# Shifting where the blocks of three operands begin in SBUF, in a two-layer trunk with experts

## The chip, the cores and the metric

The kernel runs on one core of one Trainium2 chip. The metric is the device time of one execution in microseconds (us). All times come from one profiled execution of the kernel before, and from three timed runs of it.

## The reference

Two decoder layers run over 256 tokens of width 1024, in float32. Each layer is an adaLN-modulated RMSNorm, a token mixer (latent attention and forgetting attention side by side), a gated residual, a second modulated RMSNorm, a channel mixer, and a gated residual; a final RMSNorm ends it. What matters here are the two channel mixers:

```
def swiglu(h, w_gate, w_up, w_down):
    return (jax.nn.silu(h @ w_gate) * (h @ w_up)) @ w_down

# layer 0: dense, h is (256, 1024), the hidden width is 3584
f = swiglu(h, dense_w_gate[0], dense_w_up[0], dense_w_down[0])

# layer 1: each token goes to the best 2 of 8 experts, gates is (256, 8)
for e in range(8):
    y = y + gates[:, e:e+1] * swiglu(t, w_gate[e], w_up[e], w_down[e])
```

## The kernel before, in words

**Numbers.** Every large product is made in three float32r matmuls. A float32 value is split into a part `hi` (rounded to float32r by ACT) and the rest `lo` (by DVE), and `hi*hi + hi*lo + lo*hi` is summed in PSUM. `mm3` (L392 to L395) does this for three given operands, and `wide` and `down` write it out for the experts. In `nc.tensor.matmul(out, a, b)` the second argument is the stationary operand, 128 columns of it, loaded by an own weight load, and the third is the moving operand, which streams through with 256 or 512 columns. Each matmul has its own weight load, also where two in a row load the same block.

**Weights from memory.** A `Stream` brings all weights in the order in which they are used. SP issues a DMA of up to 2048 columns into a buffer `raw` (L142), ACT makes `whi` of it (L160), DVE makes `wlo` (L181), and PE uses the two. A DMA waits until its buffer is free again, that is until `wlo` has been made of what lay there. The order is written out by hand in `early_order` and `moe_order`; `pump`, `rest`, `idle` and `get` decide how far ACT and DVE run ahead of PE.

**The dense stage** (`dense`, layer 0). The tokens, turned so that the width lies on the partitions, are `dT_hi` and `dT_lo`: 8 blocks of 256 columns each, block k for the 128 features k. For each of 28 slices of the hidden width, `column_products` makes gate and up: weight block k (128 columns of `whi` or `wlo`) is stationary and token block k (256 columns of `dT_hi` or `dT_lo`) is moving, three matmuls for each k. The first slice goes through `first_products`. Then the activations `dg_hi` and `dg_lo` are stationary and the down weights move, with 512 columns.

**The experts' stage** (`experts`, layer 1). `gather` collects up to 128 tokens of an expert with matmuls against a selection matrix and puts them, turned, into tiles `xe0` to `xe7`: tile k holds for two experts the `hi` and the `lo` block of features k, four blocks of 128 columns (512 bytes in each partition). `wide` makes gate and up in chunks of 512 hidden columns (7 chunks for each expert): here the tokens `xe` are stationary and the weights move with 512 columns; for each k there are three matmuls, `hi*whi`, `hi*wlo`, `lo*whi`. `turn` transposes the activations of a chunk (L1054) and splits them into `g_hi` and `g_lo`, four blocks of 128 columns each. `down` has block f of `g_hi` or `g_lo` stationary and the down weights moving, 6 matmuls for each f, into `ps_y` (L1071). For the last chunk of the last expert, `turn` takes tiles named `xe0` and `xe2` instead of `g_hi` and `g_lo`.

**Where tiles lie.** Pools hand out addresses in the order in which tiles are first asked for. Small unused tiles (`gap`) stand between some of them. In the built program every float32r operand, stationary or moving, begins at a multiple of 512 bytes in its partition, except half of the latent value weights (L734): their moving operand is eight runs of 64 columns, which begin at 256 bytes past such a multiple.

Of the kernel before, what the change touches and what calls it, by code (L numbers as in the profile page):

```python
# [15 lines left out]
F32R = mybir.dt.float32r  # L16
# [7 lines left out]
P = 128  # L24
D = 1024
KD = D // P
S = 256
# [9 lines left out]
NFC = FC // P  # L37
# [5 lines left out]
CAP = P  # L43
# [15 lines left out]
HELD = ((1, 2), (1, 5))  # L59
SPLIT_BUFS = 4  # L60
LAST = 2

NATURAL = ((0, 1), (2, 3), (4, 5), (6, 7))
PAIRS = ((0, 2), (1, 3), (4, 6), (5, 7))
# [175 lines left out]
def trunk_kernel(ctx: ExitStack, tc: tile.TileContext, x, c, positions, w_early, w_moe, router_w,  # L240
# [18 lines left out]
    def bank(tag, shape, name):  # L259
        return psum.tile(shape, F32, tag=tag, name=name, bufs={"A": 4, "B": 2, "C": 2}[tag])  # L260
# [223 lines left out]
    def close(l, section, acc, parts, n, table=None, spare=None, pairs=PAIRS, early=0):  # L484

        ps = [bank(tag, [P, 2, S], "ps_nt") for tag in ("BCBC" if pairs is PAIRS else "BBCC")]
        rs, dg = [], []
        for b in range(NB):  # L490
            ss = tiny.tile([P, 2], F32, name="ss", bufs=4)
            for j in range(0 if b else early):
                for c in halves:
                    parts(j, b, c)
            for i, c in enumerate(halves):
                for j in range(0 if b else early, n):
                    parts(j, b, c)
                t = scratch([P, 512], F32, "gated")
                nc.vector.tensor_mul(t, acc[b][i], rows[l, section][:, c])
                nc.vector.tensor_add(x_sb[:, b, c], x_sb[:, b, c], t)  # L500
                square_sum(x_sb[:, b, c], ss[:, i:i + 1])
                if b and not i:
                    dg.append(diag(rs[0]))
            rs.append(row_r(ss, D, "x", ws.rest if b else None))
        dg.append(diag(rs[1]))
        if table:
            nc.scalar.preload_act_table_set(table)
        sums = ws.held.pop(spare)() if spare else iter(())
        bank_was, fold_bank[0] = fold_bank[0], "A"
        for b in range(NB):  # L510
            turned(x_sb, b, dg[b], ps, pairs)
            for put in islice(sums, 1):
                ws.late.append([partial(tuple, (put,)), 2])
        fold_bank[0] = bank_was
        return ps, rs
# [43 lines left out]
    def mixer(l, pool, ps_x, loads=None, steps=None):  # L559
# [217 lines left out]
        def group_T(g, between=None):  # L777

            ps = [bank("A" if g else "B", [P, 2, S], "ps_nt") for _ in range(2)]
            for b in range(NB):  # L780
                turned(o_sb[g], b, o_dg[g][b], ps)

            def high(kk, j):
                i = 4 * g + 2 * kk + j
                nc.scalar.activation(onT_hi[:, i], ps[kk][:, j], AF.Copy, scale=vec(l, V_OUT + i, 1))

            def low(kk, j):
                i = 4 * g + 2 * kk + j
                nc.vector.scalar_tensor_tensor(onT_lo[:, i], ps[kk][:, j], vec(l, V_OUT + i, 1),
                                               onT_hi[:, i].bitcast(F32), ALU.mult, ALU.subtract)  # L790


            for kk in range(2):
                for j in range(2):
                    high(kk, j)
                for j in range(2):
                    low(kk, j)
                    if between and not kk + j:
                        between()
# [8 lines left out]
        def out_first(kd):  # L808
            if not acc:
                acc.extend([bank("A", [P, 512], "ps_w") for _ in range(2)] for _ in range(NB))  # L810
            w = ws.get()
            for b in range(NB):
                for hf in range(2):
                    out_part(kd, w, b, halves[hf], kd == 4, False)
# [22 lines left out]
        group_T(0, partial(ws.pump, 1, SPLIT_BUFS))  # L837
        for kd in range(4 - LAST):
            out_first(kd)
        last = ws.get(LAST)  # L840
        ws.settle(True)
        if l:
# [3 lines left out]
        ws.pump(2 - l, need=2)  # L846
        return close(l, 2, acc, lambda i, b, c: out_part(4 - LAST + i, last[i], b, c, False, i == LAST - 1), LAST,
                     "silu_and_others" if l == 0 else None, pairs=NATURAL if l else PAIRS)


    def dense(l, pool, ps_x):
        hT_hi = pool.tile([P, KD, S], F32R, name="dT_hi")
        hT_lo = pool.tile([P, KD, S], F32R, name="dT_lo")
        modulated_T(l, V_FFN, 4, 3, ps_x, hT_hi, hT_lo)
        acc = [[bank("A", [P, 512], "ps_d") for _ in range(2)] for _ in range(NB)]
        fold_bank[0] = "C"
        gs = {}

        def down(j, w, b, c):
            t = slice(b * P, (b + 1) * P)  # L860
            mm3(acc[b][c.start // 512], gs[j][0][:, t], gs[j][1][:, t], w[0][:, c], w[1][:, c], j == 0, j == NF - 1)

        for j in range(NF):
            if j:
                ps = bank("B", [P, 2, S], "ps_gu")
                ps = ps[:, 0], ps[:, 1]
                for i in range(2):
                    column_products(hT_hi, hT_lo, ps[i])
                    ws.idle(2)
            else:  # L870
                ps = bank("B", [P, S], "ps_gu"), bank("C", [P, S], "ps_gu")
                first_products(hT_hi, hT_lo, ps)
                ws.idle(4)
            if 0 < j < NF - LAST + 1:
                w = ws.get()
                for b in range(NB):
                    for hf in range(2):
                        down(j - 1, w, b, halves[hf])
                ws.idle(2)
            if j == NF - 1:  # L880
                ws.rest()
            s = pool.tile([P, S], F32, name="silu", bufs=2)
            nc.scalar.activation(s, ps[0], AF.Silu)
            nc.vector.tensor_mul(s, s, ps[1])
            g_hi = pool.tile([P, S], F32R, name="dg_hi", bufs=LAST + 1)
            g_lo = pool.tile([P, S], F32R, name="dg_lo", bufs=LAST + 1)
            split(g_hi, g_lo, s)
            gs[j] = (g_hi, g_lo)
        last = ws.get(LAST)
        ws.settle(True)  # L890
        ws.pump(1, need=2)
        nc.scalar.preload_act_table_set("natural_log_exp_and_others")
        fold_bank[0] = "B"
        return close(l, 5, acc, lambda i, b, c: down(NF - LAST + i, last[i], b, c), LAST, spare=(1, 2), early=LAST - 1)


    def experts(l, outer, ps_x, rs):
# [11 lines left out]
        w = outer.tile([P, 4, NB], F32, name="w")  # L909
# [6 lines left out]
        back, xe = {}, {}  # L916
# [87 lines left out]
        with tc.tile_pool(name="moe", bufs=1, reuse_waits="tile") as pool:  # L1004
            def gather(e, pk):

                xe[e], xe[e + 1] = [], []
                for k0 in range(0, KD, 2):
                    for k in range(k0, k0 + 2):
                        both = pool.tile([P, 2, 2, CAP], F32R, name=f"xe{k}")  # L1010
                        ps = bank("B", [P, 2, 2, CAP], "ps_g")
                        for i, part in enumerate((h_hi, h_lo)):
                            for b in range(NB):
                                nc.tensor.matmul(ps[:, i], part[:, b, k * P:(k + 1) * P], pk[:, b],  # L1014
                                                 start=(b == 0), stop=(b == NB - 1))
                        nc.scalar.activation(both, ps, AF.Copy)
                        for j in range(2):
                            xe[e + j].append((both[:, 0, j], both[:, 1, j]))
                    yield
# [20 lines left out]
            def turn(pend):  # L1040
                e, ch, act = pend
                g = []
                yield e, ch, g
                if (e, ch) == (E - 1, CH - 1):

                    spare = [pool.tile([P, 2, 2, CAP], F32R, name=f"xe{f}") for f in range(0, NFC, 2)]
                    groups = [(2 * i, 2 * i + 2, [t[:, 0], t[:, 1]]) for i, t in enumerate(spare)]
                else:
                    groups = [(0, NFC, [pool.tile([P, NFC, CAP], F32R, name=f"g_{w}") for w in ("hi", "lo")])]
                for f0, f1, (hi, lo) in groups:  # L1050
                    n = f1 - f0
                    ps = bank("B", [P, n, P], "ps_gt")
                    for i in range(n):
                        nc.tensor.transpose(ps[:, i], act[:, (f0 + i) * P:(f0 + i + 1) * P], ident)  # L1054
                    split(hi[:, :n], lo[:, :n], ps)
                    g += [(hi[:, i], lo[:, i]) for i in range(n)]
                    yield
# [434 lines left out]
```

## Time and profile before

| | |
|---|---|
| median of 3 runs | 1524.0 us (1523.59 to 1524.49) |
| profiled execution | 1524.38 us |
| its span, first to last instruction | 1522.2 us |
| granted TensorE clock, mean over the span | 0.995 |
| dense stage | about 155 to 390 us |
| experts' stage | about 538 to 1511 us |

PE is TensorE's matmul, PEld its weight load, DVE VectorE, ACT ScalarE, SP SyncE with the DMA queue. Matmuls are pipelined: the duration of a matmul is its latency, and the next one starts long before it ends. The pace of PE is therefore read from one start to the next, never from the duration. Where a row is merged (x2, x24), its start is that of the first matmul in it. Starts are rounded to 0.01 us, so that a pace is taken over several matmuls.

### The profile page before, as it was taken

To read this page: it belongs to the slowest core of one execution; us is meant where nothing else is said; L and a number is where in the kernel's file an instruction comes from. 1 tells how busy PE (TensorE), PEld (TensorE's weight loads), DVE (VectorE), ACT (ScalarE), POOL (GpSimd) and SP (SyncE) were. 2 spreads that over 40 slices of the span, in tenths; PEclk is the share of its full clock that TensorE was granted. 3 is DMA by queue.
4 is the path that set the end of the run, shared out by engine and by line. 5 is a ranking of instruction groups with operands and counts; after the bars stand their busy time and mean duration, and the time that the engine had idled before them with its cause. 6 is when DMAs were issued, how large, how long until landed. Compare 5 with 4: busy or idle time off the path is not lost.

```text
span 1522.2 us, 20572 instructions
## 1 busy us (share of the span) xinstructions
PE 1491.9 (98%) x7985; PEld 1277.0 (84%) x7985; DVE 1265.4 (83%) x1209; ACT 1004.9 (66%) x1068; POOL 12.6 (1%) x20
## 2 busy tenths in 40 slices
PE   8999999999999899999999999999999999999997
PEld 7988999999898678888888888888888888888885
DVE  5988877777776678899889889879889888988987
ACT  5575544444657576777677777677777777776774
POOL 1000000000000000000000000000000000000000
PEclk9999999999999999999999999999999999999999
DMA  9974778778581269999999999999999998999992
GB/s 373 412 268 166 290 276 309 287 291 299 186 291 56 84 257 363 378 364 371 366 347 348 373 367 366 371 340 347 377 370 368 373 362 324 369 372 377 360 370 91
DMA packets 68472, 481.73 MB, mean 316 GB/s; under 512 B 7953, under 2 KB 8593, under 8 KB 10770
## 3 DMA queue, kind: packets, MB, share of 16 engines
q1 hardware_dynamic: 68178, 480.33, 83.1%
q8 instruction: 63, 1.03, 0.3%
q14 instruction: 39, 0.32, 0.1%
q0 software_dynamic: 192, 0.05, 0.0%
HBM read 479.25 MB, written 1.05 MB: 316 GB/s over the span
## 4 chain that ended last, share of the span: by engine, by line
PE 63%; DVE 1%; ACT 0%; issue 0%; DVEq 0%; ACTq 0%
PE ps_y L1071 20%; PE ps_gate L1028 20%; PE ps_up L1028 19%; PE ps_gt L1054 2%; PE ps_g L1014 1%; DVE wlo L181 0%; PE ps_sc L1097 0%; PE ps_sc L1098 0%; ACT whi L160 0%; PE ps_sc L1121 0%; PE ps_b L928 0%; DVE fin L1129 0%; ACT L1154 0%; DVE gate L347 0%; ACT junk L399 0%
## 5 line engine op out<-in xcount | busy, mean ns | idle before, releaser
L181 DVE TENSOR_TENSOR wlo<-raw,whi 128x2048 fp32r<-128x2048 f32 (+1 forms) x474 | 923.8, 1975 | 62.5 <-ACT whi L160 57.2
L160 ACT ACTIVATE whi<-raw 128x2048 fp32r<-128x2048 f32 (+1 forms) x474 | 769.9, 1662 | 158.6 <-PE ps_gu L394 77.4
L1028 PE MATMUL ps_gate<-whi,xe 128*128 128x512 f32 x896 | 301.8, 396 | 0.0
L1028 PE MATMUL ps_up<-whi,xe 128*128 128x512 f32 x896 | 288.3, 390 | 0.0
L1028 PEld LDWEIGHTS ps_up<-whi,xe 128*128 128x128 f32 x896 | 168.3, 188 | 35.3
L1028 PEld LDWEIGHTS ps_gate<-whi,xe 128*128 128x128 f32 x896 | 168.3, 188 | 33.4
L1028 PE MATMUL ps_gate<-wlo,xe 128*128 128x512 f32 x448 | 175.1, 391 | 0.7 <-DVE wlo L181 0.7
L1028 PE MATMUL ps_up<-wlo,xe 128*128 128x512 f32 x448 | 174.9, 390 | 0.1
L1071 PE MATMUL ps_y<-wlo,g_hi 128*128 128x512 f32 x440 | 136.8, 389 | 0.4 <-DVE wlo L181 0.4
L1071 PE MATMUL ps_y<-whi,g_hi 128*128 128x512 f32 x440 | 136.7, 389 | 0.0
L1071 PE MATMUL ps_y<-whi,g_lo 128*128 128x512 f32 x440 | 136.6, 389 | 0.0
L393 PE MATMUL ps_gu<-dT_hi,whi 128*128 128x256 f32 x432 | 122.5, 284 | 0.0
L395 PE MATMUL ps_gu<-dT_hi,wlo 128*128 128x256 f32 x432 | 122.2, 283 | 0.0
L394 PE MATMUL ps_gu<-dT_lo,whi 128*128 128x256 f32 x432 | 122.2, 283 | 0.0
L444 ACT ACTIVATE g_hi<-ps_gt 128x512 fp32r<-128x512 f32 x55 | 33.0, 599 | 127.1 <-PE ps_gt L1054 127.1
L1028 PEld LDWEIGHTS ps_up<-wlo,xe 128*128 128x128 f32 x448 | 84.1, 188 | 19.0 <-DVE wlo L181 1.4
L1028 PEld LDWEIGHTS ps_gate<-wlo,xe 128*128 128x128 f32 x448 | 84.3, 188 | 17.0 <-DVE wlo L181 1.3
L1071 PEld LDWEIGHTS ps_y<-wlo,g_hi 128*128 128x128 f32 x440 | 82.4, 188 | 18.0 <-DVE wlo L181 1.0
L445 DVE TENSOR_TENSOR g_lo<-ps_gt,g_hi 128x512 fp32r<-128x512 f32 x55 | 37.9, 689 | 71.4 <-ACT g_hi L444 71.4
L1071 PEld LDWEIGHTS ps_y<-whi,g_lo 128*128 128x128 f32 x440 | 82.6, 188 | 17.2
L1071 PEld LDWEIGHTS ps_y<-whi,g_hi 128*128 128x128 f32 x440 | 82.3, 188 | 16.9
L393 PEld LDWEIGHTS ps_gu<-dT_hi,whi 128*128 128x128 f32 x432 | 82.8, 192 | 1.2 <-issue 0.2
(295 smaller groups left out, 1926.4 us busy)
## 6 DMA issues: line engine op xcount, KB each, us to landing
raw<-in_w_moe_dram SPq DMA_DIRECT2D x336, 1024.0 KB, 6.9
raw<-in_w_early_dram SPq DMA_DIRECT2D x114, 1024.0 KB, 6.8
raw<-in_w_early_dram SPq DMA_DIRECT2D x6, 512.0 KB, 8.6
gate<-in_ada_b_dram SPq DMA_DIRECT2D x4, 512.0 KB, 5.6
x_sb<-in_x_dram SPq DMA_DIRECT2D x1, 1024.0 KB, 7.3
out_dram<-fin SPq DMA_DIRECT2D x4, 256.0 KB, 2.0
fg<-in_final_g_dram SPq DMA_DIRECT2D x1, 512.0 KB, 4.9
cn<-in_consts_dram SPq DMA_DIRECT2D x1, 192.0 KB, 12.6
```

The source lines that it names most:

```text
L160: self.nc.scalar.activation(hi, raw, AF.Copy)
L181: self.nc.vector.tensor_sub(parts[1], raw, parts[0].bitcast(F32))
L393: nc.tensor.matmul(out_, lh, rh, start=start, stop=False)
L394: nc.tensor.matmul(out_, lh, rl, start=False, stop=False)
L395: nc.tensor.matmul(out_, ll, rh, start=False, stop=stop)
L444: nc.scalar.activation(hi, src, AF.Copy)
L445: nc.vector.tensor_sub(lo, src, hi.bitcast(F32))
L1014: nc.tensor.matmul(ps[:, i], part[:, b, k * P:(k + 1) * P], pk[:, b], start=(b == 0), stop=(b == NB - 1))
L1028: nc.tensor.matmul(ps, lh, w[:, c], start=(k == 0 and lh is xe_hi and w is hi), stop=(k == KD - 1 and lh is xe_lo))
L1054: nc.tensor.transpose(ps[:, i], act[:, (f0 + i) * P:(f0 + i + 1) * P], ident)
L1071: nc.tensor.matmul(y_ps[e][hf], lh, w[:, hf * 512:(hf + 1) * 512], start=(ch == 0 and f == 0 and lh is g_hi and w is hi), stop=(last and l ...
```

## The change

The change makes three groups of blocks begin at different places within 512 bytes. `STEP` is 16 float32 elements, 64 bytes.

- `dT_hi` and `dT_lo` get rows of 256 + 16 elements for each block, of which 256 are used. Block k then begins 64 k bytes past a multiple of 512. These are moving operands.
- Tile `xe{k}` grows from 2048 to 2560 bytes in a partition, and its four blocks begin 64 k bytes into it. All eight tiles begin at multiples of 512, so the blocks of features k begin 64 k bytes past one. These are stationary operands.
- `g_hi` and `g_lo` get rows of 128 + 16 elements, so that block f is 64 bytes further on than the one before. Each of these tiles has then 2304 bytes. In the built program `g_hi` begins at a multiple of 512 and `g_lo`, which follows it, 256 bytes past one: its blocks lie at 256, 320, 384 and 448. These are stationary operands. For the last chunk the two spare `xe` tiles are used from their beginning.

The weights `whi` and `wlo` stay at multiples of 512. The built programs have the same instructions in the same order on every engine, with the same sizes and the same waits; only addresses and strides differ.

```
+STEP = 16
...
     def dense(l, pool, ps_x):
-        hT_hi = pool.tile([P, KD, S], F32R, name="dT_hi")
-        hT_lo = pool.tile([P, KD, S], F32R, name="dT_lo")
+
+        hT_hi, hT_lo = (pool.tile([P, KD, S + STEP], F32R, name=f"dT_{w}")[:, :, :S] for w in ("hi", "lo"))
...
                     for k in range(k0, k0 + 2):
-                        both = pool.tile([P, 2, 2, CAP], F32R, name=f"xe{k}")
+                        both = pool.tile([P, 4 * CAP + KD * STEP], F32R, name=f"xe{k}")
+                        both = both[:, k * STEP:k * STEP + 4 * CAP].rearrange("p (w j s) -> p w j s", w=2, j=2)
...
-                    spare = [pool.tile([P, 2, 2, CAP], F32R, name=f"xe{f}") for f in range(0, NFC, 2)]
+                    spare = [pool.tile([P, 4 * CAP + KD * STEP], F32R, name=f"xe{f}")[:, :4 * CAP]
+                             .rearrange("p (w j s) -> p w j s", w=2, j=2) for f in range(0, NFC, 2)]
                     groups = [(2 * i, 2 * i + 2, [t[:, 0], t[:, 1]]) for i, t in enumerate(spare)]
                 else:
-                    groups = [(0, NFC, [pool.tile([P, NFC, CAP], F32R, name=f"g_{w}") for w in ("hi", "lo")])]
+                    groups = [(0, NFC, [pool.tile([P, NFC, CAP + STEP], F32R, name=f"g_{w}")[:, :, :CAP]
+                                        for w in ("hi", "lo")])]
```

## Rows read from the trace of the kernel before

**Rows 1.** The page: span, busy time by engine, chain by engine.
```profile
span 1522.2 us, 20572 instructions
PE 1491.9 (98%) x7985; PEld 1277.0 (84%) x7985; DVE 1265.4 (83%) x1209; ACT 1004.9 (66%) x1068; POOL 12.6 (1%) x20
PE 63%; DVE 1%; ACT 0%; issue 0%; DVEq 0%; ACTq 0%
```

**Rows 2.** Two stretches: us, busy by engine (x instructions), clock, DMA share, GB/s.
```profile
155.00:390.00 235.00, 234.58 (x1663) 220.67 (x1663) 180.18 (x225) 109.30 (x144) 0.00 (x0) 1.00 0.80 295
545.00:1510.00 965.00, 963.86 (x4398) 796.86 (x4397) 850.11 (x522) 701.70 (x491) 0.00 (x0) 1.00 0.93 354
```

**Rows 3.** The chain in order of time: start us, us, what (x count).
```profile
558.68 5.44 PE ps_up L1028 x24
575.48 5.46 PE ps_up L1028 x24
...
751.21 5.44 PE ps_y L1071 x24
```

**Rows 4.** Timeline of PE, dense gate and up: start us, us, instruction.
```profile
350.80 0.28 PE L395 MATMUL ps_gu<-dT_hi,wlo 128*128 128x256 f32 x1
...
352.12 0.28 PE L394 MATMUL ps_gu<-dT_lo,whi 128*128 128x256 f32 x1
```

**Rows 5.** Timeline of PE, from 256 to 512 columns and back (dense down).
```profile
347.46 0.40 PE L393 MATMUL ps_d<-whi,dg_hi 128*128 128x512 f32 x1
347.69 0.40 PE L394 MATMUL ps_d<-wlo,dg_hi 128*128 128x512 f32 x1
...
348.85 0.39 PE L393 MATMUL ps_d<-whi,dg_hi 128*128 128x512 f32 x1
...
350.21 0.28 PE L393 MATMUL ps_gu<-dT_hi,whi 128*128 128x256 f32 x1
350.32 0.28 PE L394 MATMUL ps_gu<-dT_lo,whi 128*128 128x256 f32 x1
350.44 0.28 PE L395 MATMUL ps_gu<-dT_hi,wlo 128*128 128x256 f32 x1
```

**Rows 6.** Timeline of PE, latent values, moving operand 256 bytes off.
```profile
102.12 0.39 PE L394 MATMUL ps_uv<-wlo,cq_hi 128*128 128x512 f32 x1
...
103.28 0.38 PE L746 MATMUL ps_t<-cn,pr 128*128 128x128 f32 x2
```

**Rows 7.** Line L954: duration ns min/median/max, first and last start us.
```profile
L954 PE MATMUL ps_r<-rw,rT x32: 275/275/275, 523.0 to 526.5; 128*128 128x128 f32 x32
```

**Rows 8.** Groups by shape: xcount | busy us, mean ns | idle before us.
```profile
L1028 PE MATMUL ps_gate<-whi,xe 128*128 128x512 f32 x896 | 301.8, 396 | 0.0
L1028 PE MATMUL ps_up<-wlo,xe 128*128 128x512 f32 x448 | 174.9, 390 | 0.1
L1071 PE MATMUL ps_y<-whi,g_lo 128*128 128x512 f32 x440 | 136.6, 389 | 0.0
L393 PE MATMUL ps_gu<-dT_hi,whi 128*128 128x256 f32 x432 | 122.5, 284 | 0.0
```

**Rows 9.** Waits of the DMA queue: us in total, times, longest us.
```profile
SPq L142 <- DVE wlo L181: 1123.4, 394, 19.0
```

**Rows 10.** The page's 40 slices: GB/s that the DMA engines moved.
```profile
GB/s 373 412 268 166 290 276 309 287 291 299 186 291 56 84 257 363 378 364 371 366 347 348 373 367 366 371 340 347 377 370 368 373 362 324 369 372 377 360 370 91
```

## The prediction

> **What bounds the kernel now.** I read the page first. PE is busy for 98% of the span, and the chain that ended last, which reaches back to the start of the experts' stage, is almost all PE [rows 1]. The table by stretches says the same stage by stage: in the dense stage PE is busy for 234.58 of 235 us, and in the experts' stage for 963.86 of 965, at a granted clock of 1.00, the 2.4 GHz level [rows 2]. So what one matmul costs from start to start is what these two stages cost, and nothing else that the change touches is on the path.
>
> Then I read that pace from starts. In the experts' stage 24 matmuls of 512 columns take 5.44 to 5.46 us, 226.7 ns each, for gate and up and for down alike [rows 3]. In the dense stage eleven matmuls of 256 columns take 352.12 - 350.80 = 1.32 us, 120.0 ns each [rows 4]. The difference, 106.7 ns, is what 256 columns cost. So 512 columns cost 213.3 ns, and in both shapes 13.3 ns are left over for each matmul: 226.7 - 213.3 and 120.0 - 106.7. This rest doesn't grow with the columns. It belongs to what each matmul has once, and that is its weight load, which runs while the matmul before it streams.
>
> The rest is not the same everywhere. In the dense down products the first six matmuls after the switch from 256 columns take 348.85 - 347.46 = 1.39 us, 231.7 ns each, and the next six 350.21 - 348.85 = 1.36, 226.7. On the way back the first 256-column matmul takes 350.32 - 350.21 = 0.11 us and the next 0.12 [rows 5]. The weight load and the stream therefore meet in some way that depends on how they stand to each other, and settle after a few matmuls into the pace that the stages run at. Whether that meeting is one of addresses is the question that the change asks. 13.3 ns are 32 columns of 4 bytes, 128 bytes of the moving operand's stream, twice the 64 bytes of a step.
>
> **The change part by part.** The instructions, their order, sizes and waits stay. What could change is the pace of the matmuls whose stationary or moving block is shifted, and the writing of those blocks. The writes (ACT and DVE into `dT`, `xe`, `g`) have as many elements as before, in `dT` and `g` with 64 bytes left out behind each block; they lie beside PE, and I cost them at nothing: DVE is busy for 850 of 965 us and ACT for 702 [rows 2]. Without that cover a slower `g_lo` would delay `down`, which comes a chunk later, so it has many microseconds to spare.
>
> The number of shifted matmuls, of the groups in [rows 8] (each line has its fellows): gate and up of the experts are 2 x (896 + 448) = 2688, of which blocks k = 1 to 7 are shifted, 2352. Down has 3 x 440 = 1320; `g_hi` is stationary in two thirds of them and shifted for three of four blocks, 660, and `g_lo` is shifted in all 440. Dense gate and up have 3 x 432 and 48 more in the first slice, 1344, of which 1176 are shifted.
>
> What one shift is worth no row shows for float32r at other than multiples of 512 and 256 bytes. The bounds:
> - Best: the whole rest of 13.3 ns goes. (2352 + 1100 + 1176) x 13.3 = 62 us.
> - Worst: the matmuls never settle, and run at the 231.7 ns seen after a switch: 5.0 ns more on the experts' 2688 + 1320 matmuls, 20 us, and nothing in the dense stage, where the unsettled matmul was the faster one.
> - Nothing: 0.
>
> For a start 256 bytes off there is a row: the latent values' moving operand begins there, and five matmuls take 103.28 - 102.12 = 1.16 us. The same five behind a switch with everything at multiples of 512 take 348.85 - 347.69 = 1.16 [rows 5, 6]. So a distance of 256 bytes buys nothing, and I take the blocks at 256 out: k = 4 in gate and up (336 matmuls) and in the dense stage (168), and f = 0 of `g_lo` (110). 2016 + 990 + 1008 = 4014 matmuls are left.
>
> For these I take half of the rest, 6.7 ns: it is what the one 256-column matmul with another footing saved (0.11 us against 0.12, and 106.7 + 6.7 = 113.4), it is one step of 64 bytes at the stream's pace, and it lies between nothing and all. 4014 x 6.7 = 26.9 us: 6.8 in the dense stage, 20.1 in the experts'.
>
> Is it handed back? The experts' stage would shrink from 965 to 945 us. DVE would then be busy for 850 of 945, 90%. The DMA would have to bring 354 x 965 / 945 = 362 GB/s on average; single slices of this stage already run at 378 and an early one at 412 [rows 10]. The DMA queue mostly waits for a buffer, 1123 us in total for DVE's `wlo` [rows 9], so it is the user and not the memory that sets its pace. I hand back 1 us. In all -26: the profiled execution took 1524.4 us (a span of 1522.2 and 2.2 around it, 0.4 over the median), and 1524 - 26 = 1498.
>
> The Trainium skill speaks against this. In "TensorE: Matmul & The Clock Gate", section "Step-by-step: what each phase is for", it says that PE has two independent read ports to SBUF and that loading the next weights doesn't take read bandwidth from the running matmul. By that the rest is no meeting of two reads, and the sum is 0: this is the first rival. The section "Back-to-back issue gap" there gives N/2.4 + 2.5 ns, 215.8 ns for 512 columns; this trace has 226.7, so something that this rule doesn't hold takes 10.8 ns of each. By the rule's pace as a floor the best case would be 4628 x 10.8 = 50 us.
>
> **The rivals.**
> 1. Nothing happens; the rest is a fixed price of a float32r weight load. For it: the rest is the same for all tiles, wherever they lie, and in both shapes; the 256-byte start made no difference [rows 6]; and the router's 32 matmuls, whose moving blocks begin at 32 k bytes past a multiple of 512, all have the same duration, 275 ns at the least and at the most, and take some 113 ns each [rows 7]. Against it: those are plain float32, streaming at a slower pace per column, and the rest varies behind a switch. Time: 1524.
> 2. Slower: the settled pace needs the stationary and the moving block to keep their relation from one matmul to the next. Block k changes it after every three matmuls of gate and up and every two or four of down, and the unsettled stretch behind a switch lasts about six [rows 5], so the experts' stage stays unsettled at 231.7 ns: +20 us, 1544. It decides if L1028 runs above 229 ns on average. For it: among the 512-column rows of the dense down products the settled ones are the fastest. Against it: it takes the disturbance of a switch for that of an address, and rows 6 show none.
> 3. All of the rest goes for all shifted blocks: -62 us by count, 46 of them in the experts' stage, which would then want 354 x 965 / 919 = 372 GB/s and DVE at 92.5%. That is as much as most slices reach; I hand back 10 us: 1472.
>
> **How the numbers follow.** A measurement of this kernel tells 0.2%, 3 us, from no change. Forecast (a gain of 8 to 40 us, 1498 as the middle): 0.34. Rival 3: 0.08. Rival 1, within 3 us: 0.31. Rival 2, and lesser losses of the same kind: 0.27. So faster 0.42, same 0.31, slower 0.27. The forecast's own range is 1484 to 1516. The range for 8 in 10 has to hold rival 1 and most of rival 2: 1478 to 1544 leaves out some 0.06 below and 0.11 above, where losses beyond the 5 ns lie.
>
> **What would show it.** The pace from start to start by block: in `wide`, k = 0 and 4 should stay at 226.7 ns and the other k be at 220; in the dense gate and up 113 against 120; in down `g_lo` f = 0 should be as before. If all k have the same pace as before, rival 1 holds. If k = 0 is slower too, the disturbance is carried from block to block, as in rival 2. The forecast is wrong too if the pace falls and the time doesn't: then PE must show new idle time in front of L1028 and L1071, ended by DVE's `wlo`.

## The result and the profile after

The changed kernel is slower: 1538.0 us (median of 4 runs, 1536.85 to 1540.09) against 1524.0 beside it, a ratio of 1.0093 (95% interval 1.0076 to 1.0111), +14.0 us. The forecast was 1498.

The page of the profile shows the same kernel with a slower PE. The profiled execution is the slowest of the four: its span grew by 15.6 us, and PE's busy time by 15.5. DVE and ACT, the instructions and the chain's shares are all but the same as in [rows 1].

```profile
span 1537.8 us, 20573 instructions
PE 1507.4 (98%) x7985; PEld 1277.3 (83%) x7985; DVE 1265.9 (82%) x1209; ACT 1005.0 (65%) x1068; POOL 12.6 (1%) x20
PE 64%; DVE 1%; ACT 0%; issue 0%; DVEq 0%; ACTq 0%
```

The stretches show where. The columns are those of [rows 2]; the experts' stretch is taken 15 us longer, so that it holds the same 4398 matmuls. PE is busy for all of both at the same clock, so the 15 us are a slower pace. DMA falls from 354 to 349 GB/s, because the same bytes have more time.

```profile
155.00:391.00 236.00, 235.58 (x1681) 221.00 (x1681) 181.37 (x227) 110.99 (x147) 0.00 (x0) 1.00 0.80 296
545.00:1525.00 980.00, 979.16 (x4398) 797.65 (x4397) 850.52 (x522) 702.54 (x491) 0.00 (x0) 1.00 0.92 349
```

The chain in order of time, which answers to [rows 3], gives that pace: 24 matmuls of 512 columns take 5.56 us, 231.7 ns each, in gate and up and in down, where they took 5.44 to 5.46.

```profile
576.41 5.56 PE ps_up L1031 x24
581.97 5.56 PE ps_y L1076 x24
...
610.62 5.56 PE ps_up L1031 x24
```

The dense timeline, which answers to [rows 4], has thirteen intervals in 352.56 - 351.02 = 1.54 us, 118.5 ns, where there were 120.0. It has got faster, by 1.5 ns and not by 6.7.

```profile
351.02 0.28 PE L396 MATMUL ps_gu<-dT_lo,whi 128*128 128x256 f32 x1
...
352.56 0.28 PE L397 MATMUL ps_gu<-dT_hi,wlo 128*128 128x256 f32 x1
```

The groups by shape, to be held against [rows 8], go the same two ways. These are latencies and not paces: the three 512-column groups have a mean of 2 to 4 ns more, the 256-column group 3 ns less.

```profile
L1031 PE MATMUL ps_gate<-whi,xe 128*128 128x512 f32 x896 | 305.1, 400 | 0.0
L1031 PE MATMUL ps_up<-wlo,xe 128*128 128x512 f32 x448 | 175.8, 392 | 0.0
L1076 PE MATMUL ps_y<-whi,g_lo 128*128 128x512 f32 x440 | 138.2, 393 | 0.0
L395 PE MATMUL ps_gu<-dT_hi,whi 128*128 128x256 f32 x432 | 121.3, 281 | 0.0
```

The waits show no new one. The longest wait of PE for DVE's `wlo` in front of L1031 is 0.6 us, and the DMA queue waits a little longer for its buffers than in [rows 9], since PE now takes them more slowly.

```profile
PE ps_gate L1031 <- DVE wlo L183: 0.6, 1, 0.6
SPq L144 <- DVE wlo L183: 1140.7, 394, 19.0
```

Added up from start to start over the whole trace, gate and up of the experts take 9.2 us more (2688 matmuls, 3.4 ns each), down 6.3 us more (1344, 4.7 ns each), and the dense gate and up 2.0 us less (1344, 1.5 ns each). That is +13.5 of the 15.6 us by which the span of this execution grew. Of the rest, 0.4 us lie in the dense down products and 1.7 in small products, most of them outside the two stages.

### The profile page after: what moved, and what is told of

Its sections match the earlier page's. It is cut to its first block, busy times and chain, and to the rows that moved or that the text cites. A ratio compares the mean times of both kernels' runs of the same rounds, so it can differ in the third digit from the quotient of the medians.

```text
span 1537.8 us, 20573 instructions
## 1 busy us (share of the span) xinstructions
PE 1507.4 (98%) x7985; PEld 1277.3 (83%) x7985; DVE 1265.9 (82%) x1209; ACT 1005.0 (65%) x1068; POOL 12.6 (1%) x20
## 3 DMA queue, kind: packets, MB, share of 16 engines
q8 instruction: 63, 1.03, 0.3%
## 4 chain that ended last, share of the span: by engine, by line
PE 64%; DVE 1%; ACT 0%; issue 0%; DVEq 0%; ACTq 0%
PE ps_y L1076 20%; PE ps_gate L1031 20%; PE ps_up L1031 20%; PE ps_gt L1059 2%; PE ps_g L1017 1%; DVE wlo L183 0%; PE ps_sc L1102 0%; PE ps_sc L1103 0%; PE ps_sc L1126 0%; PE ps_b L930 0%; ACT whi L162 0%; DVE fin L1134 0%; ACT L1159 0%; DVE gate L349 0%; ACT junk L401 0%
## 5 line engine op out<-in xcount | busy, mean ns | idle before, releaser
L1031 PE MATMUL ps_gate<-whi,xe 128*128 128x512 f32 x896 | 305.1, 400 | 0.0
L1031 PE MATMUL ps_up<-whi,xe 128*128 128x512 f32 x896 | 292.1, 394 | 0.0
L1031 PEld LDWEIGHTS ps_up<-whi,xe 128*128 128x128 f32 x896 | 168.2, 188 | 38.8
L1031 PEld LDWEIGHTS ps_gate<-whi,xe 128*128 128x128 f32 x896 | 168.8, 188 | 36.5
L1031 PE MATMUL ps_gate<-wlo,xe 128*128 128x512 f32 x448 | 175.8, 392 | 0.6 <-DVE wlo L183 0.6
L1031 PE MATMUL ps_up<-wlo,xe 128*128 128x512 f32 x448 | 175.8, 392 | 0.0
L1031 PEld LDWEIGHTS ps_up<-wlo,xe 128*128 128x128 f32 x448 | 84.3, 188 | 19.8 <-DVE wlo L183 1.4
L1031 PEld LDWEIGHTS ps_gate<-wlo,xe 128*128 128x128 f32 x448 | 84.6, 189 | 17.3 <-DVE wlo L183 1.0
```

Source lines behind the costliest of these rows:

```text
L1031: nc.tensor.matmul(ps, lh, w[:, c], start=(k == 0 and lh is xe_hi and w is hi), stop=(k == KD - 1 and lh is xe_lo))
```

## The experiments

The question was what in an address sets the pace. "Distance" below is the start of the stationary block minus that of the moving block, in bytes within a partition. So a moving block that begins 112 bytes further on has a distance of -112, which is 144 modulo 256. In the expectations A is the theory that a change of place from one block to the next costs (rival 2 of the prediction), B that the absolute place costs (a block that doesn't begin at a multiple of 512 bytes), C that addresses do nothing to a matmul and the time comes from the writing of the blocks, D that the distance counts, modulo 256 bytes.

**1. Places one by one.** A kernel of nothing but float32r matmuls in groups of 36 with one pair of places in each (all other work left out):

```
+    for i, (n, moves) in enumerate(TESTS):
+        for j, (s0, m0) in enumerate(moves):
+            nc.tensor.matmul(ps[:, :n], st[:, s0:s0 + P], mv[:, m0:m0 + n], ...)
```

> Only a row of float32r matmuls, 36 in each group, back to back, none waits for data; the rest of the trunk is left out. Groups differ in where the stationary block (128 columns) and the moving block (512 or 256 columns) begin. Theory A (a matmul's pace hangs on whether the relation of its start addresses to those of the matmul before stays): with any constant offset the pace settles at 226.7 ns (120.0 for 256 columns), as with none; with an offset that changes from matmul to matmul it runs unsettled at 229 to 236. Theory B (a block that doesn't begin at a multiple of 512 bytes costs more by itself): a constant offset costs the same 232. Theory C (addresses do nothing, the longer time comes from the writing side): 226.7 in all groups. Theory D (the relation of the stationary to the moving block sets the price): constant offsets of one of the two differ among each other, offsets of both by the same amount don't.

Four stretches of its timeline (start us, us from the first start to the last end, count): distance 0, distance 64, distance 256, and both blocks 64 bytes off.

```profile
16.69 4.49 PE L299 MATMUL ps_t<-mv,st 128*128 128x512 f32 x19
...
48.74 5.53 PE L299 MATMUL ps_t<-mv,st 128*128 128x512 f32 x23
...
81.66 5.60 PE L299 MATMUL ps_t<-mv,st 128*128 128x512 f32 x24
...
173.84 5.38 PE L299 MATMUL ps_t<-mv,st 128*128 128x512 f32 x23
```

With the last one's latency of 0.40 us taken off, one takes (4.49 - 0.40) / 18 = 227 ns, 233, 226 and 226. The means over the last 24 of each group, worked out from the starts (the very first group over its last 12, as its first starts are still 427 ns apart):

```
512 columns, stationary block moved by   0: 226.7   64: 233.3  128: 232.7  192: 228.9  256: 226.7
                                       320: 233.3  384: 232.1  448: 228.9
512 columns, moving block moved by      16: 231.7   64: 228.9  256: 226.7  384: 233.3  448: 233.3
both moved by                           64: 226.7  256: 226.7
stationary place 64 bytes on each time, or after every three: 231.7; 256 or 512 bytes on each time: 226.7
both places on together each time by    64: 230.5  128: 228.3  448: 231.7  256: 226.7
256 columns, stationary block moved by   0: 120.0   64: 117.8  128: 118.6  192: 117.8  256: 120.0  320: 113.3
distance 0, other widths, columns      384: 173.3  448: 206.7  480: 216.7  496: 223.3
```

For 512 columns, a moving block 64 bytes on does what a stationary one 64 bytes back does (228.9 both), 320 does what 64 does, and if both lie 64 bytes on nothing happens. So the distance counts, modulo 256 bytes, as D says. A constant 64 doesn't come back to 226.7, which A wanted, and both off by 64 costs nothing, against B. C falls too, because nothing writes these blocks while the matmuls run. The stepping pattern of the change gives 231.7, the pace of `wide` after.

The distance of a matmul's own two blocks is not all of it, however. Where both places go on together from one matmul to the next, by 64, 128 or 448 bytes, that distance is 0 throughout, and yet the matmuls run slower than 226.7 ns:

```profile
338.76 6.62 PE L299 MATMUL ps_t<-mv,st 128*128 128x512 f32 x28
...
346.83 6.56 PE L299 MATMUL ps_t<-mv,st 128*128 128x512 f32 x28
...
363.72 6.65 PE L299 MATMUL ps_t<-mv,st 128*128 128x512 f32 x28
```

These are (6.62 - 0.40) / 27 = 230 ns, 228 and 231. So a change of place does cost something, as A says, unless it is one of 256 bytes. For 256 columns one distance had two paces (117.8 at 64, 113.3 at 320), and that stays unexplained.

**2 to 4. The parts of the change alone.** Each is one part of the diff (the notes behind `#`, here and below, are not in the code):

```
+        hT_hi = pool.tile([P, KD, S + STEP], F32R, name="dT_hi")[:, :, :S]           # dense alone
+                        both = both[:, k * STEP:k * STEP + 4 * CAP].rearrange(...)   # xe alone
+    groups = [(0, NFC, [pool.tile([P, NFC, CAP + STEP], F32R, ...)[:, :, :CAP] ...   # g alone
```

> Only dT_hi and dT_lo are shifted. In the kernel with all shifts the dense gate and up run at about 118.7 ns instead of 120.0: 1344 x 1.3 = 1.8 us faster by theories A and D, 1522.2; not slower. Theory B: slower, by up to 4 us. Theory C: 1524.

1523.49 us against 1523.49, ratio 0.9997 (0.9988 to 1.0006). The dense gate and up are 1.9 us shorter in its trace, less than the time can tell: inconclusive by the time.

> Only the experts' tokens are shifted. Theory A: L1028 runs unsettled at 231.7 ns, and the groups of down that follow it settle within some six matmuls: 2688 x 4 = 10 to 12 us slower, about 1535. Theory B: 2352 of 2688 matmuls slower by 5, 12 us, and down exactly as before at 226.7 from its first matmul on. Theory C: slower only if PE shows idle time in front of L1028.

1532.71, ratio 1.0055 (1.0040 to 1.0071). In its chain gate and up have slowed, and down almost not:

```profile
564.63 5.46 PE ps_y L1075 x24
576.08 5.56 PE ps_up L1031 x24
```

> Only g_hi and g_lo are shifted. Theory A: down unsettled at about 231.5 ns, 1320 x 4.8 = 6 us slower, about 1530, and the first matmuls of gate or up behind each down slower too. Theory B: 990 x 5 = 5 us slower and gate and up as before. Theory C: slower only by idle time in front of L1071.

1530.95, ratio 1.0047 (1.0032 to 1.0062), and here only down:

```profile
559.28 5.44 PE ps_up L1030 x24
564.72 5.54 PE ps_y L1073 x24
```

The parts give +9.2, +7.5 and 0, together 16.7 against the whole's 14.0, with intervals of some 2.5 us on each. The loss is that of the two stationary operands. A slow product slows the other one only where it begins: with `xe` alone shifted, the first four matmuls of each down take 236, 228, 232 and 231 ns (medians) and the others 227, which is 1.1 us over all of down.

**5. Every 16 bytes, and bfloat16.** The same kind of kernel, with 30 in a group, each distance twice and behind different groups (the loop is that of experiment 1), and 120 matmuls of bfloat16:

```
+    for i, r in enumerate((0, 32, 64, 96)):
...
+            nc.tensor.matmul(ps, sb[:, r:r + P], mb[:, :512], start=(j == 0), stop=(j == 29))
```

> Again only matmuls, the rest of the trunk is left out. Float32r with 512 and with 256 columns, the distance of the stationary from the moving block in steps of 16 bytes from 0 to 240, each once behind matmuls of the other shape and once behind 480-column ones; then the dense stage's own pattern, 12 of 512 columns with both at multiples of 512 and 48 of 256 columns with the moving block at a constant distance; then bfloat16 at four distances. The theory so far (the price is set by the distance of the two blocks modulo 256 bytes): the same mean for a distance whatever came before, 512 columns 226.7 at 0, about 233 at 64, 128 to 233 at 128, 229 at 192; 256 columns 120.0 at 0 and lower elsewhere, 113.3 at the best. Rival (each distance has several paces and what came before chooses): the two passes differ. For bfloat16, which reads half the bytes, either the same steps at all distances or none.

512 columns ran at 233.3 ns for most distances, at 226.7 at 0, 228.9 at 192 and 228.3 at 240, in both passes alike to 0.6 ns. 256 columns ran at 120.0 at 0 and settled at 113.3 with the moving block 112 bytes on, in both passes; 32 gave 116.7, most others 117 to 120. But at some places the passes differ: 118.7 and 116.7 ns at 16 bytes, 118.8 and 117.3 at 160. There the rival of the expectation holds, that what came before chooses among several paces. The timeline shows 256 columns at 0, then at 112, and the bfloat16 matmuls at 0, 64, 128 and 192 bytes together:

```profile
273.74 3.52 PE L290 MATMUL ps_t<-mv,st 128*128 128x256 f32 x28
...
312.83 1.41 PE L290 MATMUL ps_t<-mv,st 128*128 128x256 f32 x11
...
570.42 26.07 PE L296 MATMUL ps_b<-mb,sb 128*128 128x512 bf16 x117
```

(3.52 - 0.28) / 27 = 120.0 and (1.41 - 0.28) / 10 = 113.0. The bfloat16 row has 117 records of 120 matmuls: (26.07 - 0.40) / 119 = 215.7 ns, at all four distances alike.

**6 and 7. One place for all `xe`, and two places 256 bytes apart.** In the kernel itself, A and D want opposite things of these two:

```
+                        both = both[:, STEP:STEP + 4 * CAP].rearrange(...)                 # all at 64
+                        both = both[:, k % 2 * 64:k % 2 * 64 + 4 * CAP].rearrange(...)     # odd k at 256
```

> All blocks of the experts' tokens begin 64 bytes past a multiple of 512, for every k the same. Theory A (the change from one matmul to the next costs): nothing changes from block to block, L1028 settles at 226.7 and the time is 1524. Theory D (the distance of the stationary from the moving block modulo 256 bytes sets the pace): every gate and up matmul runs at about 233.3, 2688 x 6.7 = 18 us slower, 1542: more than with all eight offsets.

1539.79 against 1524.24, ratio 1.0103 (1.0086 to 1.0120). The place no longer changes, and gate and up are slower than with the change itself: 5.60 / 24 = 233.3 ns.

```profile
559.88 5.60 PE ps_up L1031 x24
565.49 5.47 PE ps_y L1075 x24
```

> The experts' tokens of odd k begin 256 bytes past a multiple of 512, those of even k at one. Theory D: 256 bytes are a whole turn, 226.7 ns, 1523.5 to 1524. Theory A with a turn of 512 bytes, and any theory by which a block over a 512-byte boundary costs more: slower by 5 to 12 us.

1524.17, ratio 1.0002 (0.9992 to 1.0011). The place changes with each k, and nothing is lost:

```profile
575.27 5.46 PE ps_up L1031 x24
```

Both go as D says. That the change of place alone sets the price (A) falls in the kernel too.

**8 to 10. The distances that experiment 5 found for 256 columns.** `dT` at a constant 112 bytes, at 32, and at 112 together with the mixers' `hT`:

```
+        hT_hi, hT_lo = (pool.tile([P, KD * S + P], F32R, name=f"dT_{w}")[:, 28:28 + KD * S]
+                        .rearrange("p (k s) -> p k s", k=KD) for w in ("hi", "lo"))
```

> Only dT_hi and dT_lo are moved, all their blocks begin 112 bytes past a multiple of 512; the experts' stage is as before. The second row of matmuls had 256 columns at that distance settle at 113.3 ns after some 4 to 12 matmuls, in both passes, against 120.0 at 0. If the distance alone sets the pace, the dense gate and up come to about 114.5 ns, 1344 x 5.5 = 7 us faster, 1517. If the pace of 113.3 needs what came before in that row (rival), 118 to 119 ns: 1521 to 1522.

1516.96 against 1523.87, ratio 0.9953 (0.9940 to 0.9967). The dense timeline runs at (350.25 - 347.19) / 27 = 113.3 ns, and all of gate and up takes 153.9 us from start to start where it took 161.6.

```profile
span 1515.3 us, 20573 instructions
...
347.19 0.28 PE L395 MATMUL ps_gu<-dT_hi,wlo 128*128 128x256 f32 x1
...
350.25 0.28 PE L395 MATMUL ps_gu<-dT_hi,wlo 128*128 128x256 f32 x1
```

> As before it with 32 bytes, where 256 columns ran at 116.7 ns in both passes from the second matmul on: 1344 x 3.3 = 4.4 us faster, 1519.8. Rival: no gain that can be told from none.

1520.52, ratio 0.9979 (0.9970 to 0.9988): half the gain, as the 116.7 ns of experiment 5 wanted.

> dT and also the mixers' hT begin 112 bytes past a multiple of 512 (onT, in the same memory, does not). The mixers have some 600 more matmuls of 256 columns with hT moving, 5.5 ns each or 3 us, and 192 of 512 columns with hT stationary, which should go from 226.7 to about 233: 1.3 us back. With the dense stage's 7 us in all 9 us, 1515. Rival as for the dense stage alone: 1521 to 1523.

1514.18, ratio 0.9937 (0.9923 to 0.9951): faster than both kernels. `hT` is also the stationary operand of 512-column products, 96 of them; those became slower, 233 ns for 227, which takes back 0.5 us. `onT`, left at 0, is stationary in 512-column products too; whether moving it could add to the gain wasn't tried.

**11. A faster place for 512 columns?** The kernel of experiment 1 with each distance from 0 to 252 in steps of 4 bytes, and with two places in turn:

```
+    for r in range(64):
+        out.append([(512, r, 0)] * 30)
```

> Only float32r matmuls of 512 columns, the rest is left out: every distance of the stationary from the moving block from 0 to 252 bytes in steps of 4, 30 matmuls each, and then distances that alternate from one matmul to the next. Theory D as it stands (a turn of 256 bytes, 0 the best): 226.7 ns at 0 and 228 to 235 at all others. Rival: some distance lies below 226.7, as 112 bytes of the moving block does for 256 columns (113.3 against 120.0); 220.0 would be the same step of 6.7 ns, and worth 27 us in the experts' stage.

None. 226.7 ns is the least, at 0, 120, 132, 144, 156, 240, 244 and 252; the others lie between 229 and 238, and two places in turn are never below 226.7. But 144 ran at 233.3 in both passes of experiment 5, and 240 at 228.3. The first line is of experiment 5 and the second of this one, both at a distance of 144 bytes:

```profile
86.73 4.60 PE L290 MATMUL ps_t<-mv,st 128*128 128x512 f32 x19
...
265.66 4.70 PE L276 MATMUL ps_t<-mv,st 128*128 128x512 f32 x20
```

That is (4.60 - 0.40) / 18 = 233 ns and (4.70 - 0.40) / 19 = 226. So the distance alone doesn't fix the pace at every place, for 512 columns either.

**12. Both operands off by 64 in the kernel.** A 64-byte gap ahead of the split weights, so that, by the layout of the built program, 6904 of the float32r matmuls have both blocks 64 bytes past a multiple of 512:

```
+    gap(split_pool, 64)
     ws = Stream(nc, sources, pieces, raw_pool, split_pool, fold)
```

> A gap of 64 bytes ahead of the split weights moves whi, wlo, the experts' tokens, the activations and all tiles behind them, so that 6904 float32r matmuls have both blocks at 64 bytes past a multiple of 512. Theory D (only the distance between the two counts): 226.7 and 120.0 ns as before, 1524, though each of these blocks now runs over a 512-byte boundary. Theory B (a block off a multiple of 512 costs more by itself): at least the 14 us of the change.

1523.67 against 1524.35, ratio 0.9996 (0.9986 to 1.0005), and the chain has the old pace:

```profile
563.18 5.44 PE ps_y L1072 x24
574.52 5.44 PE ps_up L1029 x24
```

A constant shift of both blocks costs nothing, so B falls; 64 bytes on one side alone cost 15.6 us in experiment 6.

## Why the prediction was wrong, step by step

- **What bounds the kernel** was right. PE's pace from start to start is the time, in both stages: it makes 13.5 of the 15.6 us by which the profiled span grew.
- **"For these I take half of the rest, 6.7 ns"** is the step that failed, in its sign for the experts and in its size for the dense stage. It took one price for both shapes. The 512-column products of the experts lost 3.8 ns each on average, and the dense 256-column ones gained 1.5. For 512 columns none of the distances tried is better than 0 (experiment 11), so these shifts could only lose or do nothing. For 256 columns the 6.7 ns do exist, at 112 bytes (experiments 5 and 8), but at multiples of 64 experiment 5 has 118 to 120. The single short interval in [rows 5] that the price rested on is no sign of another place: in experiment 5 the first 256-column matmul behind 512-column ones takes 113 ns, too, and the next 119 and 120, with every block at a multiple of 512 bytes. It belongs to the switch, and that a constant 112 bytes holds the same pace is luck.
- **This rest doesn't grow with the columns** was read from two widths. At distance 0 experiment 1 has 206.7 ns for 448 columns and 216.7 for 480; at the prediction's 106.7 ns for 256 columns that leaves 20.0 and 16.7 ns, where 256, 384 and 512 columns leave 13.3. So the rest is no fixed price of which a share could be taken.
- **The rest belongs to the weight load and is a matter of addresses**: that it is one of addresses is shown, since only the places were changed in experiments 6, 8 and 12. That it is the reading of the next stationary block that meets the stream is only argued: no run separates the load from the stream. That a change of both places costs at distance 0 (experiment 1) fits it, because the next stationary block is then not at distance 0 from the running stream.
- **256 bytes buy nothing** was right as such, in experiments 1 and 7. The count built on it was not: with the whole change, the blocks at 0 and 256 bytes are slower too. Over 46 rounds of up the three matmuls of k = 0 take 235, 228 and 229 ns, and those of k = 4 take 236, 228 and 229 (medians), where all took 227.
- **Rival 1**, no effect at all, falls for float32r by +1.03% in experiment 6. The rule that was named beside it, in the Trainium skill, "TensorE: Matmul & The Clock Gate", section "Step-by-step: what each phase is for", is that loading the next weights takes no read bandwidth from the running matmul. The bfloat16 row agrees with it, as its 215.7 ns don't depend on the four places tried; the float32r rows, whose pace depends on how the two blocks lie to each other, speak against it, though no run shows the reading itself. In the Trainium skill, "TensorE: Matmul & The Clock Gate", the section "Back-to-back issue gap" gives N/2.4 + 2.5 ns for an isolated matmul, 215.8 ns for 512 columns: the bfloat16 row agrees, the float32r rows with 226.7 at the best don't.
- **Rival 2** had the direction and the pace: 231.7 ns to the digit, by 4008 x 5.0 = 20 us. Its mechanism is at most a part of the cause. The change of relation doesn't set the price, as a constant 64 is worse still (233.3) and a change by 256 costs nothing. But the constant distances 0, 64, 128 and 192 would average 230.4 and not 231.7, and the slower k = 0 is the sign that the prediction had named for this rival: something does carry over from block to block. That the pace agreed to the digit is luck in part, since the rival took it from a switch of widths. The size came out at +15.5 and not +20, and the dense stage gave 2.0 back.
- **I hand back 1 us** stays untested, as the experts' stage got longer and there was nothing to hand back. No new wait appeared: PE's longest wait for `wlo` in front of L1031 is 0.6 us.
- The range, 1478 to 1544, holds the time because rival 2 was kept within it.

## What to carry to other kernels

Where PE's pace is the time and the operands are float32r, look at how the stationary and the moving blocks lie to each other: for 512 columns keep their distance at a multiple of 256 bytes, and for 256 columns try moving blocks that all begin 112 bytes further on than the stationary ones, separately for each shape. A price read at one odd interval of one shape is not the price of another shape; measure the pace of the exact pair of places, in the order of the kernel, in a small kernel before the whole layout is moved. Here a constant place that had been measured gained 7 us, and a pattern that only spread the places lost 14.

## What the runs showed of the hardware

- The pace of float32r matmuls depends on the distance of the two operands' blocks, for 512 columns between 226.7 and 238 ns. For 512 columns, constant places a multiple of 256 bytes apart gave 226.7 each time. A constant shift of both blocks does nothing (226.7 with both 64 bytes off), but a place that changes from one matmul to the next costs also at distance 0 (230.5 ns by 64 bytes each time).
- 256 columns have one of their slowest paces, 120.0 ns, where 512 have their fastest, at distance 0; with the moving block 112 bytes on they run at 113.3.
- One distance can have two paces (256 columns: 117.8 at 64, 113.3 at 320; 512 columns at 144: 233.3 and 226.7), by what came before or by something that these runs don't tell apart.
- bfloat16 matmuls of 512 columns run at 215.7 ns at any of four distances (0, 64, 128, 192 bytes).
- Why 256 bytes are a whole turn, and what meets in between, stays open.
